# Values and output gates of three heads as one 512-column projection, with the modulation sums kept in their result tiles

## The chip, the cores and the metric

One NeuronCore of one Trainium2 chip runs the whole program. The metric is the device time of one execution in microseconds (us); less is better.

## What is computed

One layer of a backbone over 1024 latent and 256 context tokens, model width 1024, one batch element. `mod` is a vector of six parts of 1024 numbers made from the conditioning vector.

```python
mod = silu(c) @ w_mod + b_mod                 # sh1, sc1, ga1, sh2, sc2, ga2
hc  = modulate(ctx, g_mix, csh1, csc1);  hx = modulate(x, g_mix, sh1, sc1)
p   = h @ w_in                                # q, k, v, o and gates of 4 heads, tokens of hc and hx
# per head: two chunked mLSTM scans (forward, backward), started from the context's state
hn  = h * rsqrt(mean(h*h) + EPS) * gain
y   = (hn * sigmoid(o)) @ w_out;  x = x + ga1 * y
x   = x + ga2 * conv_glu(modulate(x, g_ffn, sh2, sc2))
out = rmsnorm(x, g_final)
```

The head's keys and queries are 128 wide, its values `v` and output gates `o` 256 wide. `o` is needed for the 8 latent chunks alone, `v` for all 10.

## The kernel before

Tokens are cut into 10 chunks of 128: two of context (0, 1) and eight latent (2 to 9). Every product of fp32 numbers is made of three matmuls (`mm3`, L84 to L87: high by high on L85, low by high on L86, high by low on L87), so each weight block is first split into a high and a low half: a copy on ScalarE (L80) and a subtraction on VectorE (L81).

The buffers matter here. Split weights live in tiles with the tag `w`, 8 buffers. Their unsplit sources, and the rows of `w_mod`, land in tiles with the tag `raw`, 3 buffers (`load_raw`, L72); a load into a `raw` tile waits on SyncE's queue (SP) until the tile's last reader is done, and the loads behind it in that queue wait too. Projections accumulate in PSUM tiles `pj`, 2 buffers.

`proj_v` (L278 to L306) makes the values of a head chunk by chunk: 24 matmuls of 256 columns into `pv`, then a copy `vh` (L297, ScalarE) and a rest `vl` (L298, VectorE). `proj_o` makes the output gates of the eight latent chunks in the same way into `po`, with a tanh (L334) and +1 (L335). `proj_qk` makes keys (`pk`) and queries (`pq`) with the roles swapped, 512 tokens at a time. For head 0 the values carry the gate columns along (272 columns), and `gate_rows` turns them into the scan's coefficients: `grp` (L350), `cp` (L387), `bp`, `mp`, `op` on TensorE with VectorE work between, ended by `cco` (L427). `mlstm` then makes per head the two scans: transposed keys `kt`, their scaled halves `kh`/`kl` (L458, L459), chunk states `dc`, scores `s`, outputs `nm`, the normalised `ha` (L545, L551) and its transpose `yp` (L559).

`weave` runs one head's `mlstm` and lets it draw, at some 27 points, units of other matrix work: the values that were left over of this head (`VLATE` = 4 tiles), its output gates, and the next head's keys, queries and first values. Beside every second unit one row of `w_mod` is summed: `mod_sum` (L587 to L596) adds 8 rows of 1024 columns, each times a scalar (L594, VectorE), into a `w` tile that starts at zero. Four such chunks (m3, m4, m2, m5) are made during heads 0 to 2. During head 3 `first_pair` fills in: the gates of head 3, then the output projection of heads 0 and 1 (`opa`) with its weights `wor` (multiplied by ga1, L690, and split) and the y of the heads read back (`load_y`, `split_y` L699/L700), and the residual add (`add_x2`, L711) into x tiles loaded on L727.

The order of instructions on each engine comes out of a scheduler that works on this program with a cost model of its own; the code's order is its input.

Of the kernel before, what the change touches and what calls it, by code (L numbers as in the profile page):

```python
# [9 lines left out]
F32 = mybir.dt.float32  # L10
F32R = mybir.dt.float32r
# [28 lines left out]
def backbone(ctx, tc, x, c, ctxt, c_ctx, w_mod, b_mod, g_mix, g_ffn, w_in, b_gate,  # L40
# [48 lines left out]
    def kp(src):  # L89
        return src.rearrange("(k p) n -> p k n", p=P)  # L90
# [40 lines left out]
    def pj(name):  # L131
        return ps.tile([P, 512], F32, tag="pj", bufs=2, name=name)
# [145 lines left out]
    def proj_v(h, wts=None):  # L278

        hd[h]["v"] = vv = {}  # L280
        if wts is None:
            wh, wl = wcols(OFF_V + h * DV, DV, f"wv{h}_")
            n = DV
        else:
            n = VG
            wh = [a[:, k * n:(k + 1) * n] for a, _ in wts for k in range(4)]
            wl = [a[:, k * n:(k + 1) * n] for _, a in wts for k in range(4)]
        for tt in range(NCH) if wts else BWD:
# [11 lines left out]
            if n == VG:  # L300

                for d, j in ((0, tt), (1, BWD.index(tt))):
                    V.tensor_tensor(out=gt.rearrange("p (y d h) c -> p y d h c", y=2, d=2)[:, :, d, :, j],
                                    in0=p_[:, DV:VG].rearrange("p (y d h) -> p y d h", y=2, d=2)[:, :, d, :],
                                    in1=bgate.rearrange("p (y d h) -> p y d h", y=2, d=2)[:, :, d, :], op=ALU.add)
            yield  # L306

    def proj_qk(h):
# [275 lines left out]
        yield 1  # L584
        readout(LCH - 1)

    def mod_sum(chunk, name, use):  # L587

        acc = wtile(name, F32)
        V.memset(acc, 0.0)  # L590
        nc.sync.dma_start(out=acc[0:1, :], in_=b_mod[:, chunk * D:(chunk + 1) * D])
        for k in range(KT):
            r_ = load_raw(w_mod[k * P:(k + 1) * P, chunk * D:(chunk + 1) * D], f"{name}r{k}")
            V.scalar_tensor_tensor(out=acc, in0=r_, scalar=sct[:, k, 0:1], in1=acc, op0=ALU.mult, op1=ALU.add)  # L594
            yield
# [57 lines left out]
    def along(units, side):  # L653

        for i, _ in enumerate(units):
            if i % 2:
                next(side, None)
            yield

    mods = chain(mod_sum(3, "m3", mod_cols(h2col)), mod_sum(4, "m4", mod_cols(s2col, gffn)),  # L660
                 mod_sum(2, "m2", mod_bcast(ga1)), mod_sum(5, "m5", mod_bcast(ga2)))
    VLATE = 4
    late = iter(())
    for h in range(H - 1):
        nv = proj_v(h + 1)
        fill = along(chain(late, proj_o(h), proj_qk(h + 1), islice(nv, NCH - VLATE)), mods)
        hd[h]["o"] = []
        weave(mlstm(h), fill)
        late = nv
    run(mods)  # L670
# [43 lines left out]

    def first_pair():

        po = proj_o(H - 1)
        yield from islice(po, 4)
        ws = load_wout(0, 0) + load_wout(1, 0)
        yield from po  # L720
        yr = [load_y(0, 0), load_y(0, 1), load_y(1, 0)]
        open_ap()
        ys = [split_y(0, 0, yr[0]), split_y(0, 1, yr[1]), split_y(1, 0, yr[2])]
        ys.append(split_y(1, 1, load_y(1, 1)))
        for tt in range(LCH):
            t_ = atile(f"x2_{tt}")
            nc.sync.dma_start(out=t_, in_=x[tt * P:(tt + 1) * P, :])  # L727
            x2.append(t_)
        for hf in range(2):
            if hf:  # L730
                ws = load_wout(0, 1) + load_wout(1, 1)
            for tt in range(LCH):
                p_ = pj(f"opa_{tt}_{hf}")
                out_mm(p_, tt, ys, ws, True, True)
                add_x2(tt, hf, p_)
                yield
                if hf and tt == 1:
                    wb[1][0] = load_wout(3, 0)
                    wb[0][0] = load_wout(2, 0)

    fill = chain(late, first_pair())
    hd[H - 1]["o"] = []
    weave(mlstm(H - 1), fill)
    y2 = [split_y(2, f, load_y(2, f)) for f in range(2)]
    wb[1][1] = load_wout(3, 1)
# [435 lines left out]
```

## Time and profile before

| | |
|---|---|
| time, three runs | 1227.0, 1227.14, 1228.77 us, median 1227.14 us |
| profiled execution | 1226.6 us, of it a span of 1224.8 us in the trace |
| TensorE (PE) busy | 1190.1 us, 97% of the span, 6395 instructions |
| VectorE (DVE) busy | 887.1 us, 72% |
| ScalarE (ACT) busy | 507.0 us, 41% |
| GpSimd (POOL) busy | 76.6 us, 6% |
| granted TensorE clock, mean | 0.997 of full speed |

How to read it: the span is one profiled execution from first to last instruction. Busy means that an instruction of the engine is under way. In the rows further down, "idle before" stands in square brackets with the instruction that ended the wait, DVE instructions of one engine may overlap by some 0.1 us, and the duration of a matmul is its latency: matmuls overlap, so their pitch is read from start to start.

### The profile page before, as it was taken

What the parts mean: (1) busy time and instruction counts of PE and PEld (TensorE: products, weight loads), DVE (VectorE), ACT (ScalarE), POOL (GpSimd) and SP (SyncE); (2) the same over time, 40 slices, a digit from 0 to 9 for tenths busy, and PEclk for the clock granted to TensorE, in tenths of its full rate; (3) what the DMA queues carried; (4) which work ended last, traced back from release to release, by engine and by line L of the source; (5) the groups of instructions that cost most, each with busy time, mean ns of one, the idle gap of its engine ahead of it and who ended that gap; (6) DMA issues with size and microseconds to landing.
All of it is one profiled execution on the core that took longest, in us unless ns stands there. A gap on an engine that the chain in (4) does not pass through costs nothing. (4 is left out here: it accounts for less than half of the span.)

```text
span 1224.8 us, 17206 instructions
## 1 busy us (share of the span) xinstructions
PE 1190.1 (97%) x6395; PEld 1009.7 (82%) x6395; DVE 887.1 (72%) x1560; ACT 507.0 (41%) x911; POOL 76.6 (6%) x202
## 2 busy tenths in 40 slices
PE   8999999999999999999899999999999999999996
PEld 1788999988998998887678888888888888888885
DVE  3777584776465358657998878788888878986787
ACT  3853354353345335337443333333233344445452
POOL 0100011011001001002500000000000000000011
PEclk9999999999999999999999999999999999999999
DMA  8625252445211115142133222143535469625423
GB/s 322 216 70 157 70 147 86 130 125 155 75 55 59 44 44 223 53 155 104 51 104 103 68 87 96 59 149 128 204 121 189 138 233 401 224 93 167 163 69 120
DMA packets 120020, 160.99 MB, mean 131 GB/s; under 512 B 7932, under 2 KB 81916, under 8 KB 119936
## 3 DMA queue, kind: packets, MB, share of 16 engines
q1 hardware_dynamic: 119936, 159.89, 38.9%
q8 instruction: 50, 0.82, 0.3%
q14 instruction: 34, 0.28, 0.1%
HBM read 125.22 MB, written 34.64 MB: 131 GB/s over the span
## 5 line engine op out<-in xcount | busy, mean ns | idle before, releaser
L912 ACT ACTIVATE t<-gt,cols 128x1024 f32<-128x1024 f32 x22 | 27.4, 1245 | 62.6 <-DVE gt L810 62.6
L810 DVE TENSOR_TENSOR e<-e,p 128x512 f32<-128x512 f32 x66 | 45.1, 685 | 8.4 <-PE p L87 8.3
L810 DVE TENSOR_TENSOR gt<-e,p 128x512 f32<-128x512 f32 x66 | 45.1, 685 | 3.2 <-PE p L87 3.0
L918 ACT ACTIVATE t<-t 128x1024 f32<-128x1024 f32 x22 | 23.4, 1062 | 49.1 <-DVE t L915 49.0
L124 POOL TENSOR_SCALAR fms<-fms 128x1 f32<-128x1 f32 x8 | 3.8, 472 | 607.8 <-PE pa L87 584.3
L551 DVE SCALAR_TENSOR_TENSOR ha<-ha,hms,so 128x256 f32<-128x256 f32 x32 | 15.5, 485 | 33.7 <-POOL hms L125 32.1
L85 PE MATMUL po<-wo_0h,hxh 128*128 128x256 f32 x128 | 37.3, 292 | 0.0
L298 DVE TENSOR_TENSOR vl<-pv,vh 128x256 fp32r<-128x256 f32 x40 | 16.8, 421 | 28.2 <-ACT vh L297 28.0
L85 PE MATMUL pv<-wv_0h,hxh 128*128 128x256 f32 x120 | 34.6, 289 | 2.5 <-DVE vl L298 2.5
L913 DVE SCALAR_TENSOR_TENSOR t<-gt,cols,t 128x960 f32<-128x960 f32 x22 | 26.8, 1217 | 13.3 <-ACT t L912 13.3
L87 PE MATMUL po<-wo_1l,hxh 128*128 128x256 f32 x128 | 36.3, 283 | 0.0
L86 PE MATMUL po<-wo_1h,hxl 128*128 128x256 f32 x128 | 36.2, 283 | 0.0
L85 PE MATMUL po<-wo_1h,hxh 128*128 128x256 f32 x128 | 36.2, 283 | 0.0
L86 PE MATMUL po<-wo_0h,hxl 128*128 128x256 f32 x128 | 36.2, 282 | 0.0
L87 PE MATMUL po<-wo_0l,hxh 128*128 128x256 f32 x128 | 36.2, 282 | 0.0
L85 PE MATMUL pk<-hxh,wk_0h 128*128 128x512 f32 (+1 forms) x96 | 34.3, 358 | 0.0
L85 PE MATMUL p<-bt,av 128*128 128x512 f32 x88 | 34.2, 389 | 0.0
L86 PE MATMUL p<-bt,av 128*128 128x512 f32 x88 | 34.2, 389 | 0.0
L87 PE MATMUL p<-bt,av 128*128 128x512 f32 x88 | 34.2, 389 | 0.0
L86 PE MATMUL pk<-hxh,wk_0l 128*128 128x512 f32 (+1 forms) x96 | 34.2, 356 | 0.0
L87 PE MATMUL pk<-hxl,wk_0h 128*128 128x512 f32 (+1 forms) x96 | 34.0, 355 | 0.0
L87 PE MATMUL pv<-wv_0l,hxh 128*128 128x256 f32 x120 | 34.0, 283 | 0.0
(1031 smaller groups left out, 4247.9 us busy)
## 6 DMA issues: line engine op xcount, KB each, us to landing
rg<-in_f_w_up_dram SPq DMA_DIRECT2D x24, 512.0 KB, 4.3
rv<-in_f_w_up_dram SPq DMA_DIRECT2D x22, 512.0 KB, 3.6
actd<-t SPq DMA_DIRECT2D x22, 512.0 KB, 3.1
dr<-in_f_w_down_dram SPq DMA_DIRECT2D x44, 256.0 KB, 5.1
dr<-sums SPq DMA_DIRECT2D x44, 256.0 KB, 2.9
dr<-actd SPq DMA_DIRECT2D x33, 256.0 KB, 5.1
mr<-in_w_mod_dram SPq DMA_DIRECT2D x16, 512.0 KB, 6.4
sr<-actd SPq DMA_DIRECT2D x11, 512.0 KB, 6.7
```

Of the source, the lines that this page charges most:

```text
L85: T.matmul(ps, ah, bh, start=first, stop=False)
L86: T.matmul(ps, al, bh, start=False, stop=False)
L87: T.matmul(ps, ah, bl, start=False, stop=last)
L124: G.tensor_scalar(out=ms, in0=ms, scalar1=mult / n, scalar2=mult * EPS, op0=ALU.mult, op1=ALU.add)
L298: V.tensor_tensor(out=vl[:, 0:DV], in0=p_[:, :DV], in1=vh[:, 0:DV].bitcast(F32), op=ALU.subtract)
L551: V.scalar_tensor_tensor(out=ha, in0=ha, scalar=ms[:, 1:2], in1=so[i], op0=ALU.mult, op1=ALU.mult)
L810: V.tensor_tensor(out=out_, in0=a_, in1=b_, op=op)
L912: S.activation(out=t_, in_=gate, func=AF.Identity, scale=wcv[:, NFF + ff:NFF + ff + 1], bias=bcv[:, ff:ff + 1])
L913: V.scalar_tensor_tensor(out=t_[:, GRID_W:], in0=gate[:, :SEQ - GRID_W], scalar=wcv[:, ff:ff + 1], in1=t_[:, GRID_W:], op0=ALU.mult, op1=A ...
L918: S.activation(out=t_, in_=t_, func=AF.Silu)
```

## The change

Heads 1 to 3 get `proj_vo` in place of `proj_v` and `proj_o`: one weight block of 512 columns per k holds the head's value columns and its gate columns side by side. For the eight latent chunks 24 matmuls of 512 columns write one `pv` tile, whose first half becomes `vh`/`vl` and whose second half the gate `so`; for the two context chunks it stays at 256 columns. The weights arrive in four `raw` tiles of two loads each (`vor`) and are split into `vo_0` to `vo_3`, which take all eight `w` tiles. Six of the ten tiles are made a head ahead (`EARLY`), the other four, cut in two units each, in the head's own `mlstm`. Head 0 stays as it was. `mod_sum` adds up in `ga1` and `ga2` instead of a `w` tile. `first_pair` loses its eight units of `proj_o`.

```diff
+    def proj_vo(h):
+        hd[h]["v"], hd[h]["o"] = {}, [None] * LCH
+        wts = []
+        for kh in range(KT // 2):
+            r_ = raw_tile(f"vor{h}_{kh}")
...
+            for i, off in enumerate((OFF_V, OFF_O)):
+                nc.sync.dma_start(out=r3[:, :, i * DV:(i + 1) * DV],
+                                  in_=kp(w_in[kh * 2 * P:(kh + 1) * 2 * P, off + h * DV:off + (h + 1) * DV]))
+            h_, l_ = split(r_, f"vo{h}_{kh}")
...
+        for tt in BWD:
+            n = VO if tt >= 2 else DV
+            p_ = pj(f"pv{h}_{tt}")
+            for k in range(KT):
+                mm3(p_[:, :n], hxh[k][:, sl], hxl[k][:, sl], wts[k][0][:, :n], wts[k][1][:, :n], k == 0, k == KT - 1)
+                if k == 3 and tt >= 2:
+                    yield
...
+            S.copy(vh[:, 0:DV], p_[:, :DV])
+            V.tensor_tensor(out=vl[:, 0:DV], in0=p_[:, :DV], in1=vh[:, 0:DV].bitcast(F32), op=ALU.subtract)
+            if tt >= 2:
+                o_ = hp.tile([P, DV], F32, tag="so", bufs=8, name=f"so{h}_{tt}")
+                S.activation(out=o_, in_=p_[:, DV:], func=AF.Tanh, scale=0.5)
+                V.tensor_scalar(out=o_, in0=o_, scalar1=1.0, scalar2=None, op0=ALU.add)
...
-    def mod_sum(chunk, name, use):
-        acc = wtile(name, F32)
+    def mod_sum(chunk, name, use, acc):
         V.memset(acc, 0.0)
...
-    VLATE = 4
+    EARLY = 6
     late = iter(())
     for h in range(H - 1):
-        nv = proj_v(h + 1)
-        fill = along(chain(late, proj_o(h), proj_qk(h + 1), islice(nv, NCH - VLATE)), mods)
-        hd[h]["o"] = []
+        nv = proj_vo(h + 1)
+        if h == 0:
+            hd[0]["o"] = []
+            late = proj_o(0)
+        fill = along(chain(late, proj_qk(h + 1), islice(nv, 2 + 2 * (EARLY - 2))), mods)
         weave(mlstm(h), fill)
...
     def first_pair():
-        po = proj_o(H - 1)
-        yield from islice(po, 4)
         ws = load_wout(0, 0) + load_wout(1, 0)
-        yield from po
+        yield
```

The program order moves with it. Three places are shown; names are those of the code, numbers behind a name only tell two tiles of one name apart, and the code lines of the changed kernel are some 30 further down (its sums are on L625, its `kl` on L491, the values' `vl` of head 0 on L294 and of the others on L331).

The first place is VectorE while the last two chunks of head 0's values are made and the gate chain begins (`it`, `ff` are its first copies, which need `gt` and TensorE's `grp`). Before:

```order
L298 TENSOR_TENSOR vl_8_928<-pv_8_902,vh_8_927 128x256
L303 TENSOR_TENSOR gt<-pv_8_902,bgate 128x2x4 x2
L81 TENSOR_TENSOR wo_0l<-wo_r_1206,wo_0h 128x1024
L81 TENSOR_TENSOR wo_1l<-wo_r_1212,wo_1h 128x1024
L298 TENSOR_TENSOR vl_9_961<-pv_9_935,vh_9_960 128x256
L303 TENSOR_TENSOR gt<-pv_9_935,bgate 128x2x4 x2
L352 COPY it<-grp 40x256
```

And with the change:

```order
L625 SCALAR_TENSOR_TENSOR ga_92<-m3r_1288,vec,ga_92 128x1024
L294 TENSOR_TENSOR vl_8_928<-pv_8_902,vh_8_927 128x256
L298 TENSOR_TENSOR gt<-pv_8_902,bgate 128x2x4 x2
L625 SCALAR_TENSOR_TENSOR ga_92<-m3r_1383,vec,ga_92 128x1024
L81 TENSOR_TENSOR wo_0l<-wo_r_1206,wo_0h 128x1024
L294 TENSOR_TENSOR vl_9_961<-pv_9_935,vh_9_960 128x256
L298 TENSOR_TENSOR gt<-pv_9_935,bgate 128x2x4 x2
L81 TENSOR_TENSOR wo_1l<-wo_r_1212,wo_1h 128x1024
L384 COPY it<-grp 40x256
```

The eight sums of m3, which stood behind `cco`, now stand before and within the gate chain: two ahead of its first copy, six more before `cco`. The loads of rows 1288, 1383 and 1466 follow each other through one `raw` tile.

The second place is VectorE at the turn from head 0 to head 1: the last `ha` of head 0, and `kl` of head 1's first chunks, which the first state `dc` waits for. Before:

```order
L551 SCALAR_TENSOR_TENSOR ha_7_2369<-ha_7_2369,hms_7_2372,so_7_1559 128x256
L298 TENSOR_TENSOR vl_5_2436<-pv_5_2410,vh_5_2435 128x256
L459 SCALAR_TENSOR_TENSOR kl_1_0_2395<-kt_1_0_2392,cco,kh_1_0_2394 128x128
L459 SCALAR_TENSOR_TENSOR kl_1_1_2401<-kt_1_1_2398,cco,kh_1_1_2400 128x128
L459 SCALAR_TENSOR_TENSOR kl_1_2_2444<-kt_1_2_2441,cco,kh_1_2_2443 128x128
```

And with the change:

```order
L583 SCALAR_TENSOR_TENSOR ha_7_2343<-ha_7_2343,hms_7_2346,so_7_1558 128x256
L331 TENSOR_TENSOR vl_7_2365<-pv_7_2307,vh_7_2364 128x256
L625 SCALAR_TENSOR_TENSOR ga_91<-m2r_2971,vec,ga_91 128x1024
L336 TENSOR_SCALAR so_7_2370<-so_7_2370 128x256
L625 SCALAR_TENSOR_TENSOR ga_91<-m2r_3059,vec,ga_91 128x1024
L331 TENSOR_TENSOR vl_6_2409<-pv_6_2373,vh_6_2408 128x256
L491 SCALAR_TENSOR_TENSOR kl_1_0_2427<-kt_1_0_2424,cco,kh_1_0_2426 128x128
```

Two sums stand ahead of `kl`. The next head's `wk_r` and `wq_r` sit in two of the three `raw` tiles there, until `vo_0` and `vo_1` give `w` tiles back; rows 2707, 2875, 2971 and 3059 follow each other through the third.

The third place is VectorE in the middle of head 1, where `vo_3` of head 2 is split. Before, the second half of head 2's value weights stood among other work (`wv_1l`); with the change:

```order
L625 SCALAR_TENSOR_TENSOR ga_92<-m5r_3703,vec,ga_92 128x1024
L556 TENSOR_TENSOR wl_5_3085<-ee_5_3076,wh_5_3084 128x256
L505 SCALAR_TENSOR_TENSOR cf_5_3102<-cf_4_3018,bco,dc_0_5_3098 128x258
L571 SCALAR_TENSOR_TENSOR dn_3_3104<-nm_3_3089,cco 128x2
L557 TENSOR_TENSOR wi_6_3207<-wi_6_3207,qT_1594 128x256
L573 TENSOR_TENSOR dn_3_3104<-nm_3_3089,dn_3_3104 128x2
L547 SCALAR_TENSOR_TENSOR ee_7_3307<-mb_0_3_3208,cco,zmask 128x128
L574 RECIPROCAL dn_3_3104<-dn_3_3104 128x2
L547 SCALAR_TENSOR_TENSOR ee_7_3307<-mb_1_0_3210,cco,zmask 128x128
L625 SCALAR_TENSOR_TENSOR ga_92<-m5r_3764,vec,ga_92 128x1024
L577 SCALAR_TENSOR_TENSOR ha_3_3108<-nm_3_3089,dn_3_3104,ha_3_3108 128x256
L81 TENSOR_TENSOR vo_3l<-vor_3_3151,vo_3h 128x1024
```

`vo_3l` is needed by the 21st of 24 matmuls of the first value tile of head 2 (`pv_1`), and stands behind row 3703, the sixth of eight rows (3189, 3295, 3382, 3462, 3528, 3703, 3837, 4005) that go through one `raw` tile in turn.

## Rows read from the trace of the kernel before

**Rows 1.** The stage of heads 0 and 1, busy time of each engine (share of clock, DMA last)

```profile
110.00:200.00 90.00, 89.14 (x638) 84.03 (x637) 59.22 (x142) 38.97 (x106) 7.14 (x31) 1.00 0.43 130
```

**Rows 2.** Timeline of PE, two streams: 512 columns (pq) and 256 columns (po)

```profile
103.95 0.39 PE L85 MATMUL pq<-hxh,wq_0h 128*128 128x512 f32 x1
...
109.16 0.39 PE L87 MATMUL pq<-hxl,wq_0h 128*128 128x512 f32 x1
...
452.69 0.28 PE L85 MATMUL po<-wo_0h,hxh 128*128 128x256 f32 x1
...
458.32 0.28 PE L87 MATMUL po<-wo_1l,hxh 128*128 128x256 f32 x1
```

**Rows 3.** Waits of PE from 90 to 520 us: total, times, longest

```profile
PE pv L85 <- DVE vl L298: 2.5, 2, 2.0
PE cp L387 <- DVE gs L382: 1.3, 1, 1.3
PE dc L85 <- DVE cb L473: 0.9, 1, 0.9
PE yp L559 <- DVE ha L551: 0.8, 1, 0.8
```

**Rows 4.** Timeline of SP's queue, loads of w_mod (x2, x3: several issues in one row)

```profile
71.77 11.63 SPq L72 DMA_DIRECT2D m3r<-in_w_mod_dram  x3
...
284.67 5.15 SPq L72 DMA_DIRECT2D m5r<-in_w_mod_dram  x2
...
291.82 0.33 SPq L72 DMA_DIRECT2D m5r<-in_w_mod_dram  x1
...
299.08 0.33 SPq L72 DMA_DIRECT2D m5r<-in_w_mod_dram  x1
```

**Rows 5.** Timeline of DVE: the sums that take those loads

```profile
288.17 1.29 DVE L594 SCALAR_TENSOR_TENSOR m<-m5r,vec,m 128x1024 f32<-128x1024 f32 x1 [1.02 <-DMA m5r<-in_w_mod_dram]
...
297.77 1.28 DVE L594 SCALAR_TENSOR_TENSOR m<-m5r,vec,m 128x1024 f32<-128x1024 f32 x1 [2.34 <-DMA m5r<-in_w_mod_dram]
...
303.34 1.28 DVE L594 SCALAR_TENSOR_TENSOR m<-m5r,vec,m 128x1024 f32<-128x1024 f32 x1 [3.16 <-DMA m5r<-in_w_mod_dram]
```

**Rows 6.** Groups of DVE instructions, 90 to 520 us: busy, mean ns, idle before

```profile
L594 DVE SCALAR_TENSOR_TENSOR m<-m5r,vec,m 128x1024 f32<-128x1024 f32 x8 | 10.3, 1283 | 7.8 <-DMA m5r<-in_w_mod_dram 7.8
...
L81 DVE TENSOR_TENSOR wv_0l<-wv_r,wv_0h 128x1024 fp32r<-128x1024 f32 x3 | 3.7, 1224 | 0.4 <-PE po L86 0.3
```

**Rows 7.** Timeline of DVE at five places

```profile
83.29 0.17 DVE L303 TENSOR_TENSOR gt<-pv,bgate 128x8 f32<-128x8 f32 x1
...
205.43 0.48 DVE L551 SCALAR_TENSOR_TENSOR ha<-ha,hms,so 128x256 f32<-128x256 f32 x1 [1.55 <-POOL hms L125]
...
207.41 0.35 DVE L459 SCALAR_TENSOR_TENSOR kl<-kt,cco,kh 128x128 fp32r<-128x128 f32 x1 [1.16 <-ACT kh L458]
...
469.69 0.68 DVE L711 TENSOR_TENSOR x<-x,opa 128x512 f32<-128x512 f32 x1
...
512.80 0.48 DVE L551 SCALAR_TENSOR_TENSOR ha<-ha,hms,so 128x256 f32<-128x256 f32 x1 [1.54 <-POOL hms L125]
```

**Rows 8.** Timeline of PE at five places

```profile
83.61 0.27 PE L350 MATMUL grp<-ident,gt 128*40 128x128 f32 x1
...
205.97 0.33 PE L559 MATMUL yp<-ident,ha 128*128 128x128 f32 x1 [0.81 <-DVE ha L551]
...
207.95 0.28 PE L86 MATMUL dc<-vh,kl 128*128 128x258 f32 x1
...
508.74 0.28 PE L87 MATMUL nm<-vl,wh 128*128 128x258 f32 x1
...
588.47 0.68 PE L85 MATMUL p<-ba,ag2h 128*128 128x512 f32 x1 [3.89 <-ACT ag2h L80]
```

**Rows 9.** Windows behind a stop of PE, as rows 1

```profile
588.00:590.00 2.00, 1.53 (x4) 1.25 (x5) 2.00 (x2) 1.98 (x4) 1.08 (x1) 0.66 0.00 0
590.00:592.00 2.00, 2.00 (x7) 1.52 (x6) 2.00 (x5) 0.00 (x0) 0.00 (x0) 0.50 0.00 0
```

More of the change, by code (lines that the diff above doesn't have):

```diff
@@ L276, in backbone, with proj_v @@
     hd = [dict() for _ in range(H)]
-    def proj_v(h, wts=None):
+    def proj_v(h, wts):
         hd[h]["v"] = vv = {}
[L281 to L288, printed above, removed]
+        n = VG
+        wh = [a[:, k * n:(k + 1) * n] for a, _ in wts for k in range(4)]
+        wl = [a[:, k * n:(k + 1) * n] for _, a in wts for k in range(4)]
+        for tt in range(NCH):
             sl = slice(tt * P, (tt + 1) * P)
@@ L299, in proj_v @@
             vv[tt] = vh, vl
[L300 to L305, printed above, removed]
+            for d, j in ((0, tt), (1, BWD.index(tt))):
+                V.tensor_tensor(out=gt.rearrange("p (y d h) c -> p y d h c", y=2, d=2)[:, :, d, :, j],
+                                in0=p_[:, DV:VG].rearrange("p (y d h) -> p y d h", y=2, d=2)[:, :, d, :],
+                                in1=bgate.rearrange("p (y d h) -> p y d h", y=2, d=2)[:, :, d, :], op=ALU.add)
@@ new lines, in proj_v @@
+            yield
+    VO = 2 * DV
+    def proj_vo(h):
[3 more added lines that the diff above has]
+            r_ = raw_tile(f"vor{h}_{kh}")
+            r3 = r_.rearrange("p (k n) -> p k n", k=2)
+            for i, off in enumerate((OFF_V, OFF_O)):
+                nc.sync.dma_start(out=r3[:, :, i * DV:(i + 1) * DV],
+                                  in_=kp(w_in[kh * 2 * P:(kh + 1) * 2 * P, off + h * DV:off + (h + 1) * DV]))
+            h_, l_ = split(r_, f"vo{h}_{kh}")
+            wts += [(h_[:, k * VO:(k + 1) * VO], l_[:, k * VO:(k + 1) * VO]) for k in range(2)]
+        for tt in BWD:
+            sl = slice(tt * P, (tt + 1) * P)
+            n = VO if tt >= 2 else DV
[4 more added lines that the diff above has]
+                    yield
+            vh = vp.tile([P, VG], F32R, tag="vh", bufs=NCH, name=f"vh{h}_{tt}")[:, :DV + 2]
+            vl = vp.tile([P, VG], F32R, tag="vl", bufs=NCH, name=f"vl{h}_{tt}")[:, :DV + 2]
+            G.memset(vh[:, DV:].bitcast(F32), 1.0)
+            G.memset(vl[:, DV:].bitcast(F32), 0.0)
+            S.copy(vh[:, 0:DV], p_[:, :DV])
+            V.tensor_tensor(out=vl[:, 0:DV], in0=p_[:, :DV], in1=vh[:, 0:DV].bitcast(F32), op=ALU.subtract)
+            hd[h]["v"][tt] = vh, vl
+            if tt >= 2:
+                o_ = hp.tile([P, DV], F32, tag="so", bufs=8, name=f"so{h}_{tt}")
+                S.activation(out=o_, in_=p_[:, DV:], func=AF.Tanh, scale=0.5)
+                V.tensor_scalar(out=o_, in0=o_, scalar1=1.0, scalar2=None, op0=ALU.add)
+                hd[h]["o"][tt - 2] = o_
@@ L658, in along @@
             yield
-    mods = chain(mod_sum(3, "m3", mod_cols(h2col)), mod_sum(4, "m4", mod_cols(s2col, gffn)),
-                 mod_sum(2, "m2", mod_bcast(ga1)), mod_sum(5, "m5", mod_bcast(ga2)))
-    VLATE = 4
+    mods = chain(mod_sum(3, "m3", mod_cols(h2col), ga2), mod_sum(4, "m4", mod_cols(s2col, gffn), ga2),
+                 mod_sum(2, "m2", mod_bcast(ga1), ga1), mod_sum(5, "m5", mod_bcast(ga2), ga2))
+    EARLY = 6
     late = iter(())
     for h in range(H - 1):
-        nv = proj_v(h + 1)
-        fill = along(chain(late, proj_o(h), proj_qk(h + 1), islice(nv, NCH - VLATE)), mods)
-        hd[h]["o"] = []
+        nv = proj_vo(h + 1)
[3 more added lines that the diff above has]
+        fill = along(chain(late, proj_qk(h + 1), islice(nv, 2 + 2 * (EARLY - 2))), mods)
         weave(mlstm(h), fill)
@@ L715, in first_pair @@
     def first_pair():
-        po = proj_o(H - 1)
-        yield from islice(po, 4)
         ws = load_wout(0, 0) + load_wout(1, 0)
-        yield from po
+        yield
         yr = [load_y(0, 0), load_y(0, 1), load_y(1, 0)]
@@ L741, in backbone @@
     fill = chain(late, first_pair())
-    hd[H - 1]["o"] = []
     weave(mlstm(H - 1), fill)
```

## The prediction, made before the changed kernel ran

> **What bounds the kernel now.** I read four views. The windows by stage come first: in the stage of heads 0 and 1 TensorE is busy 89.14 of 90 us [rows 1], so whatever it is spared shows in the time, and so does every new wait of it. The timeline of TensorE gives the pitch of its matmuls [rows 2]. The list of its waits says what stops it now: 5.5 us between 90 and 520 us, all of them behind VectorE [rows 3]. The timelines of SP's queue and of VectorE show why VectorE is late: sums of rows of `w_mod` wait for a load [rows 4 to 6]. The sum below is made against the profiled execution, 1226.6 us; the median of the runs is 0.5 above it. A difference of 0.2%, 2.45 us, is about what a measurement of this kernel can tell.
>
> **Fewer matmuls.** Eight chunks of three heads need 24 matmuls of 512 columns in place of 48 of 256: 576 pairs become single ones. The 256-column stream has 48 matmuls from 452.69 to 458.32, 47 steps of 0.1198 us; the 512-column stream 24 from 103.95 to 109.16, 23 steps of 0.2265 us [rows 2]. A pair costs 0.2396, so each gives back 0.0131, and 576 give **7.5 us**, all on the path of TensorE by rows 1; I take 7.4, since four more steps into a tile change weights at a yield. Nothing else bounds it from below but a pitch as long as the pair's, no gain.
> The Trainium skill, page "TensorE: Matmul & The Clock Gate", section "Back-to-back issue gap", gives an isolated matmul a gap of N/2.4 + 2.5 ns, by which a pair costs 215.8 + 2.5 + 2.5 against 215.8 + 2.5 and the change gives back 576 x 2.5 ns, an estimate of 1.4 us. The trace differs: 13.1 ns a pair.
>
> **Edits at nothing.** ScalarE and VectorE do the same instructions; tanh and +1 of a chunk come right behind its `vh` and `vl`. SP has four loads of 256 KB per head more, beside an idle queue. The store of the gate maxima now stands behind the `vor` loads on SP, some 8 us later; its readers are needed by the first scores, for which TensorE has gates of head 0 and states to do first. The memsets that move to the start are off the path.
>
> **Waits that go.** The sums of m3 and m5 stand elsewhere now, the turn to head 1 has more filler, so the 2.5, 1.3, 0.9 and 0.8 us of rows 3 go: **-5.5 us**. Their causes come back at other places:
>
> **A load and its sum as a link.** Row for row, the sums of a chunk now share one `raw` tile in turn at the three places shown with the change. A load can start only when the sum before it is done. From issue to the waiting sum it takes 3.50 us (284.67 to 288.17), 4.26 (299.08 to 303.34) or 5.95 (291.82 to 297.77) [rows 4, 5]. I take the middle one, 4.26; with 1.28 for the sum [rows 6] a link is 5.57 us. VectorE works in order, so all behind such a sum waits too.
>
> *First place, gates.* The load of row 1288 starts at 71.77 as now [rows 4], lands at 76.1 and is summed by 77.4. Row 1383 lands at 81.7, is summed by 83.0, and then come the split of `wo_0` (1.22), `vl_9` and the gates: done at 84.8, where now it is 83.5 (83.29 and two of 0.17) [rows 7]. TensorE stands at `grp` three matmuls of 512 columns earlier than now, 83.61 - 0.68 = 82.9 [rows 8]: a stop of 1.9. Six more sums (7.7) and a split (1.22) lie within the chain that follows; it has 1.9 us more of idle stretches to hide them in at each table load of ScalarE, and `cp` comes 22 matmuls later in TensorE's order. Following both, TensorE waits 1.1 at `cp` and 0.4 at `bp`. Together **3.4**; with loads of 3.50 I get 1.3, with 5.95 about 10.
>
> *Second place, the turn to head 1.* Now `ha` of the last chunk starts at 205.43 and `kl` at 207.41, 1.98 later [rows 7], and the state `dc` with it at 207.95 [rows 8]. With the change `vl_7`, a sum, a load, a sum and `vl_6` lie between: 0.4 + 0.4 + 1.28 + 4.26 + 1.28 + 0.4 = 8.0, which is 6.0 more. Against it stands that `ha` is ready before TensorE asks for `yp_7`: between `nm_7` and `yp_7` lie 36 matmuls of 512 columns, 8.2 us, while the chain from `nm_7` to the end of `ha` took 4.5 in head 3 (508.74 to 512.80 and 0.48) [rows 7, 8]. But VectorE has thirteen sums (16.7) beside its own work there and hardly idles, so I leave 1.1 of the 3.7. Price **4.9**; ends 6.0 - 0.8 - 3.7 = 1.5 and 6.0 + 1.7 = 7.7.
>
> *Third place, `vo_3` in head 1.* From the end of sum 3189, which comes at `nm_0`, to that of 3703 are five links, 27.9; the eleven rows to the end of `vo_3l`, a sum and a split [rows 6] and nine of some 0.25, take 4.6: 32.5. TensorE has 72 matmuls of 512 columns (16.3), 44 of 256 (5.3) and four steps of scores, `nm` and `dc` (13 or 14 matmuls of up to 258 columns, 1.6 each at 0.12) up to the 21st matmul of `pv_1`, less 1.4 that passed before: 27. Price **5.5**; with loads of 3.50 VectorE's own work sets it, 3.0; with 5.95 up to 13.
>
> *`vo_3` in heads 0 and 2*, without sums: its `w` tiles come free with the last `pq` matmul, then a copy on ScalarE and 1.22 [rows 6] against 20 matmuls of 0.12: 0.4 each, **0.8**; ends 0 and 2.4.
>
> *Hand-over to `opa`.* The gate tiles of head 3 lay among its first scores; now its last value tile is followed by the splits of `wor` and of four y at once. The first residual add came 11.4 us after the last `po` matmul (458.32, 469.69) [rows 2, 7]; two more splits, 2.4, stand before it, and the x loads behind both `wor` loads on SP start some 2 us later. TensorE has no other work: **2.0**, ends 0 (all beside) and 6.0, a whole load of 5.95.
>
> *End of head 3.* Eight fill units are gone, so one `opa` tile is left behind `nm_7` where there were three: 12 x 0.2265 = 2.7 against the 4.5 of the chain, to which a split of y (1.22) is added. **3.0**, ends 1.8 and 4.5.
>
> *Clock.* Behind a stop of 3.89 us [rows 8] the granted clock was 0.66 and then 0.50 of full, its lower level of 1.2 GHz, for 2 us each [rows 9]: 0.7 + 1.0 = 1.7 us of work lost. The second and third stop are longer: **3.4**; ends 0 and 5.1.
>
> **Sum.** -7.4 - 5.5 + 3.4 + 4.9 + 5.5 + 0.8 + 2.0 + 3.0 + 3.4 = +10.1: 1236.7, on the runs' median **1237 us**, slower by 0.8%. All low ends: -12.9 + 7.6 = -5.3, 1222. The high ends together pass 1260, but they don't meet.
>
> **Rivals.** *Short stops.* The sum crosses zero when the three places cost 12.9 - 5.8 = 7.1 us together instead of 13.8, and no clock falls. With loads of 3.50 and VectorE ahead at the turn they cost 1.3 + 1.5 + 3.0, and the time is 1226.6 - 12.9 + 11.6 = 1225.3, 1226 on the median; with the low ends of the rest too it is 1222. For it: the row of 3.50. Against it: the two other rows, and that two loads now often run side by side. I give 0.15 to the stretch within 0.2% and 0.10 to faster.
> The Trainium skill, page "DMA: Bandwidth & Descriptors", section "Anatomy of one DMA", has about 2.0 us and bytes / 436e9 s per transfer, an estimate of 3.2 us for 512 KB, by which this rival would hold. Rows 4 and 5 show none as short.
>
> *The sums are covered.* VectorE may be far enough ahead of TensorE that the three places stop nothing, as most of the 7.8 us that the m5 sums wait now do no harm [rows 3, 6]. Left are 0.8, 2.0 and 3.0: 1226.6 - 12.9 + 5.8 = 1219.5, with the median 1220. Against it: `kl` and `vo_3l` are needed within some 2 us. 0.05.
>
> *Long loads.* At 5.95 the three places alone cost 31, and the time passes 1249: 0.08.
>
> *No gain from width.* If one of 512 columns cost the pair's time, only the waits stay: 1237 + 7.4 = 1244. Against it: rows 2. 0.03. The Trainium skill's issue gap, above, comes near this: an estimate of 1243.
>
> That the matmuls don't go is ruled out by the order: TensorE has 576 fewer.
>
> **How the numbers follow.** The forecast's own case, 1230 to 1249, has 0.59. Slower: 0.59 + 0.08 + 0.03 = 0.70; within 0.2%: 0.15; faster: 0.10 + 0.05 = 0.15. The range from 1222 to 1249 leaves out some 0.08 on each side. The likeliest case alone is 1230 to 1249.
>
> **What would show it.** Right: `pv` of 512 columns at a pitch of 0.2265; TensorE's waits grow from 5.5 to some 20 us, of which `grp`, `dc` behind `kl` at the turn to head 1 and `pv` behind `vo_3l` in head 1 are over 1.5, 3 and 3 us; VectorE's waits of `ga` for m3, m2 and m5 rows some 20 us in all. Wrong: `kl` of head 1 within 3 us behind `ha`; sums that wait less than in rows 6; no lower clock behind the stops.

## The result, and the profile after

| | before | with the change |
|---|---|---|
| median of the runs beside each other | 1227.07 us (4) | 1235.93 us (4: 1233.52, 1234.41, 1237.46, 1239.06) |
| ratio | | 1.0071, 95% interval 1.0054 to 1.0087 |
| profiled execution, its span | 1226.6, 1224.8 us | 1233.52, 1231.7 us |
| TensorE matmuls in the trace | 6395 | 5819 |
| granted clock, mean of the profiled execution | 0.997 | 0.990 |

Slower by 0.7%, where 0.8% was forecast: 1235.9 against 1237. The profiled execution is the fastest of the four, so the account below is of 6.9 us and not of 8.9. From the page's first part, of the changed kernel (busy us, share of the span, instructions):

```profile
PE 1190.1 (97%) x5819; PEld 981.8 (80%) x5819; DVE 888.2 (72%) x1560; ACT 508.8 (41%) x911; POOL 71.6 (6%) x202
```

TensorE's busy time is what it was, 1190.1 us, with 576 matmuls fewer. That looks as if the wider matmuls had brought nothing. They did, as the starts of one value tile of 512 columns show (timeline of TensorE, head 1's values made beside head 0; the first column is the start, the second the latency):

```profile
198.03 0.39 PE L85 MATMUL pv<-vo_2h,hxh 128*128 128x512 f32 x1
198.26 0.39 PE L86 MATMUL pv<-vo_2h,hxl 128*128 128x512 f32 x1
...
203.25 0.39 PE L87 MATMUL pv<-vo_1l,hxh 128*128 128x512 f32 x1
```

23 steps in 5.22 us, 0.227 each. Over the nine whole tiles of this kind that nothing interrupts the mean is 0.2277, and over the 21 uninterrupted 256-column tiles (`pv`, `po`) of before it is 0.1198, 0.2395 a pair. So each pair that became one matmul gave back 0.0118 us, 576 of them **6.8 us**. The busy time hides this, because time at the lower clock is busy time too.

Now the waits of TensorE between 60 and 530 us, which answer to [rows 3] (total, times, longest):

```profile
PE yp L591 <- DVE ha L583: 3.2, 1, 3.2
PE dc L86 <- DVE kl L491: 3.1, 1, 3.1
PE nm L566 <- DVE ha L577: 2.5, 2, 1.4
PE opa L85 <- DVE x L744: 2.2, 1, 2.2
PE opb L85 <- DVE yl L602: 1.2, 1, 1.2
PE cp L419 <- DVE gs L414: 0.7, 1, 0.7
...
PE pv L87 <- DVE vo_3l L81: 0.6, 1, 0.6
...
PE grp L382 <- DVE gt L298: 0.4, 1, 0.4
PE opa L86 <- DVE yl L733: 0.2, 1, 0.2
```

Together with the two lines not shown (0.7 and 0.5) this list comes to 15.3 us. The list of before over the same stretch comes to 7.2: the four lines of [rows 3], the same 0.7 and 0.5, and 0.5 at `opa`. That is **+8.1**. Nearly all of it stands behind VectorE, and in new places: head 1's first state (`dc` behind `kl`), the end of head 3 (`yp`, then `opb`), the hand-over to `opa`.

The third item is the clock. Windows of the changed kernel in four stretches (busy of each engine, then granted clock, DMA share, GB/s), as in [rows 9]:

```profile
466.00:468.00 2.00, 1.61 (x5) 1.32 (x6) 2.00 (x7) 0.41 (x1) 0.00 (x0) 0.78 1.03 420
468.00:470.00 2.00, 2.00 (x6) 1.51 (x6) 1.32 (x7) 0.78 (x2) 0.00 (x0) 0.50 1.02 418
...
526.00:528.00 2.00, 2.00 (x6) 1.58 (x5) 1.15 (x3) 1.09 (x2) 0.00 (x0) 0.50 0.80 233
...
596.00:598.00 2.00, 2.00 (x6) 1.52 (x6) 2.00 (x4) 0.71 (x2) 0.00 (x0) 0.50 0.00 0
...
608.00:610.00 2.00, 2.00 (x6) 1.54 (x5) 2.00 (x4) 0.00 (x0) 0.00 (x0) 0.50 0.68 205
```

A window at 0.50 is at the lower level, 1.2 GHz, and loses 1 us of work. With the windows beside them the four stretches lose 1.7, 1.7, 3.4 and 1.7 us, 8.5 together; before lost 1.7 at one place in the same range. **+6.8**, at most: 0.9 of the 3.4 lies within a stop that lasts to 595.20, where there was no work to lose.

Only half of it stands beside the new stops of head 3, though. The last two stretches lie in `conv_glu`, which the change does not touch. TensorE waits 3.9 us for `ag2h` there in both kernels; the fall around that stop took 3.4 us before and 6.8 us in this execution, and the wait that follows it is longer (first line before, second with the change):

```profile
PE p L86 <- DVE ag2l L81: 0.9, 1, 0.9
PE p L86 <- DVE ag2l L81: 3.4, 1, 3.4
```

Why that fall was longer is open; the profiled executions of held_apart and held_more, below, have the long fall without this wait.

The three items and the waits outside 60 to 530 us close the account of the two profiled executions. All waits of TensorE in the lists over the whole spans come to 24.5 us before and 31.1 after, +6.6 (so 1.5 less outside 60 to 530 us: 2.5 more at `ag2l`, 4.0 less at several others). Then -6.8 + 6.6 + 6.8 = +6.6, and the spans differ by 6.9. With the 0.9 taken off, 1.2 us stay unaccounted for.

### The profile page after: what moved, and what is told of

The parts are those of the page before. It is cut to its first block, busy times and chain, and to the rows that moved or that the text cites. A ratio compares the mean times of both kernels' runs of the same rounds, so it can differ in the third digit from the quotient of the medians.

```text
span 1231.7 us, 16096 instructions
## 1 busy us (share of the span) xinstructions
PE 1190.1 (97%) x5819; PEld 981.8 (80%) x5819; DVE 888.2 (72%) x1560; ACT 508.8 (41%) x911; POOL 71.6 (6%) x202
## 4 chain that ended last, share of the span: by engine, by line
PE 49%; DVE 3%; ACT 0%; POOL 0%; issue 0%; DVEq 0%; POOLq 0%; ACTq 0%
PE p L86 11%; PE p L87 11%; PE p L85 11%; PE pa L85 3%; PE pa L86 3%; PE pa L87 3%; PE pb L87 2%; PE pb L85 2%; PE pb L86 2%; DVE bt L823 1%; DVE dr L1131 0%; DVE bs L840 0%; DVE bu L823 0%; DVE at0l L81 0%; DVE dr L840 0%
## 5 line engine op out<-in xcount | busy, mean ns | idle before, releaser
L943 DVE SCALAR_TENSOR_TENSOR t<-gt,cols,t 128x960 f32<-128x960 f32 x22 | 26.7, 1216 | 13.4 <-ACT t L942 13.3
L331 DVE TENSOR_TENSOR vl<-pv,vh 128x256 fp32r<-128x256 f32 x30 | 12.5, 418 | 28.2 <-ACT vh L330 28.2
L549 ACT ACTIVATE wi<-mb,bco 128x128 f32<-128x128 f32 x64 | 23.6, 398 | 15.4 <-PE nm L566 15.3
L85 PE MATMUL nm<-vh,wh 128*128 128x258 f32 x64 | 29.9, 467 | 0.0
L330 ACT CAST vh<-pv 128x256 fp32r<-128x256 f32 x30 | 11.1, 370 | 43.1 <-PE pv L87 42.8
L491 DVE SCALAR_TENSOR_TENSOR kl<-kt,cco,kh 128x128 fp32r<-128x128 f32 x44 | 14.9, 346 | 17.7 <-ACT kh L490 17.7
L576 ACT ACTIVATE ha<-nm,dn 128x256 f32<-128x256 f32 x32 | 15.1, 473 | 29.7 <-DVE dn L574 29.6
L945 DVE SCALAR_TENSOR_TENSOR t<-gt,cols,t 128x960 f32<-128x960 f32 x22 | 26.7, 1212 | 0.0
L840 DVE TENSOR_TENSOR sa<-rv 128x512 f32<-128x512 f32 x22 | 15.1, 688 | 15.0 <-DMA rv<-in_f_w_up_dram 15.0
L86 PE MATMUL pq<-hxh,wq_0l 128*128 128x512 f32 x64 | 25.2, 394 | 0.0
```

Of the source, the lines that this page charges most:

```text
L85: T.matmul(ps, ah, bh, start=first, stop=False)
L86: T.matmul(ps, al, bh, start=False, stop=False)
L491: V.scalar_tensor_tensor(out=kl, in0=tp[:, c0:c0 + P], scalar=wc, in1=kh.bitcast(F32), op0=ALU.mult, op1=ALU.subtract)
L549: S.activation(out=wi[:, d, :], in_=mrow_, func=AF.Exp, scale=-1.0, bias=mpco[:, cc:cc + 1])
L576: S.mul(ha, nm[:, 0, :DV], dn[:, 0, :])
L840: V.tensor_tensor(out=out_, in0=a_, in1=b_, op=op)
```

## Where the waits come from

The turn from head 0 to head 1, VectorE of the changed kernel (start, duration; in brackets the idle time before it), to be held against [rows 7]:

```profile
210.94 0.48 DVE L583 SCALAR_TENSOR_TENSOR ha<-ha,hms,so 128x256 f32<-128x256 f32 x1 [1.55 <-POOL hms L125]
211.35 0.42 DVE L331 TENSOR_TENSOR vl<-pv,vh 128x256 fp32r<-128x256 f32 x1
211.98 1.28 DVE L625 SCALAR_TENSOR_TENSOR ga<-m2r,vec,ga 128x1024 f32<-128x1024 f32 x1 [0.21 <-DMA m2r<-in_w_mod_dram]
...
217.77 1.29 DVE L625 SCALAR_TENSOR_TENSOR ga<-m2r,vec,ga 128x1024 f32<-128x1024 f32 x1 [4.30 <-DMA m2r<-in_w_mod_dram]
...
219.31 0.60 DVE L491 SCALAR_TENSOR_TENSOR kl<-kt,cco,kh 128x128 fp32r<-128x128 f32 x2
```

and TensorE, which waits for that `kl`:

```profile
219.71 0.39 PE L86 MATMUL dc<-vh,kl 128*128 128x258 f32 x1 [3.11 <-DVE kl L491]
```

From `ha` to `kl` it is 8.4 us, 1.98 before. The chain is the forecast one: a sum ends at 213.26, only then can the load into the same `raw` tile start, and the next sum has its data at 217.77, 4.5 later. `kl` itself needs no load; it stands behind the sum on an engine that works in order.

The hand-over and the end of head 3 have another cause. SP's queue, VectorE and TensorE of the changed kernel at the hand-over, one fence each:

```profile
456.29 1.81 SPq L72 DMA_DIRECT2D wor<-in_a_w_out_dram  x2
458.19 6.43 SPq L758 DMA_DIRECT2D x<-in_x_dram  x8
```

```profile
465.65 0.69 DVE L744 TENSOR_TENSOR x<-x,opa 128x512 f32<-128x512 f32 x1 [2.53 <-DMA x<-in_x_dram]
```

```profile
462.18 0.70 PE L566 MATMUL nm<-cf,wi 128*128 128x258 f32 x2 [1.39 <-DVE ha L577]
...
466.39 0.50 PE L85 MATMUL opa<-wow_0h,yh 128*128 128x512 f32 x1 [2.24 <-DVE x L744]
...
523.78 0.44 PE L591 MATMUL yp<-ident,ha 128*128 128x128 f32 x2 [3.24 <-DVE ha L583]
525.44 0.79 PE L85 MATMUL opb<-wow_0h,yh 128*128 128x512 f32 x1 [1.22 <-DVE yl L602]
```

The x tiles are asked for behind the loads of `wor` and arrive 7.5 us later; no gate tile is left to fill that time. The 1.39 at `nm` just before has four splits of y (1.2 us each, from 452.14 on) ahead of `ha` on VectorE. At the end of head 3 nothing but one `opa` tile covers the chain from `nm_7` to `yp_7`.

## The experiments

All were timed in five rounds beside the kernel before. Its median there was 1226.7 (narrow to head3_apart), 1227.2 (the three held kernels) and 1229.3 us (the last two), so kernels of different groups are compared by their ratios to it (0.001 is 1.2 us). Diffs are against the changed kernel unless it is said otherwise.

**1. narrow: what the width is worth.** Only the matmuls of `proj_vo` are cut in two again; order, loads, tiles and all else stay.

```diff
-                mm3(p_[:, :n], hxh[k][:, sl], hxl[k][:, sl], wts[k][0][:, :n], wts[k][1][:, :n], k == 0, k == KT - 1)
+                for c0 in range(0, n, DV):
+                    cs = slice(c0, c0 + DV)
+                    mm3(p_[:, cs], hxh[k][:, sl], hxl[k][:, sl], wts[k][0][:, cs], wts[k][1][:, cs],
+                        k == 0 and c0 == 0, k == KT - 1 and c0 + DV == n)
```

> The changed kernel with each 512-column matmul of the joined projection cut into two of 256 columns on the same weights; all else as in the changed kernel, so 576 matmuls come back. If the width saves what the two streams of the trace of before show (0.0131 us a pair), this is slower than the changed kernel by up to 7.5 us: 1241 to 1244, less the part in which TensorE would have stood waiting anyway (the stop before dc at the turn to head 1 should shrink from 3.1 to about 1 us, as TensorE comes later). If a wide matmul saves only 2.5 ns a pair, as an isolated one would by the rule cited in the prediction, it is 1236 to 1238.

Measured 1241.13 us, ratio 1.0112 (1.0098 to 1.0125), 0.0041 or 5.0 us above the change; the profiled spans are 7.9 apart (1239.6 and 1231.7). In its trace the twelve uninterrupted runs of 48 value matmuls step by 0.1198 us, the change's nine whole tiles by 0.2277: 2 x 0.1198 - 0.2277 = 0.0119, times 576 is 6.9. So the wider matmul gives back some 5 to 8 us of time. One part of the expectation failed: the stop before `dc` did not shrink to 1 us, it stayed at 3.0. TensorE came later to the turn, but so did the `ha` at which VectorE's chain begins (212.05 instead of 210.94). The prediction's figure stands, and the 1.4 us that it had worked out from the Trainium skill, page "TensorE: Matmul & The Clock Gate", section "Back-to-back issue gap", does not.

**2. noload: the links of load and sum.** The sums take a tile that is resident anyway, so no load stands in their way; the kernel leaves out the loads and with them the real values of the later modulation.

```diff
-            r_ = load_raw(w_mod[k * P:(k + 1) * P, chunk * D:(chunk + 1) * D], f"{name}r{k}")
+            r_ = hxl[k][:, 0:D].bitcast(F32)
```

> The changed kernel with the 32 sums of the later modulation reading a resident tile in place of a freshly loaded row of w_mod: the loads are left out, the sums stay on VectorE. If the loads through one raw tile make the new stops of heads 0 and 1, the waits of TensorE at cp, nm, dc (3.1) and pv in heads 0 and 1 go, some 5.5 us in all, and the time is 1229 to 1231; the stops at the hand-over to opa and at the end of head 3 stay. If VectorE's own work with the sums makes them, dc still waits over 2 us and the time stays above 1234.

Measured 1228.49, ratio 1.0011 (1.0001 to 1.0021): 0.0060 or 7.4 us below the change, 0.5 below the range expected. Its longest waits of TensorE from 60 to 530 us:

```profile
PE yp L591 <- DVE ha L583: 3.2, 1, 3.2
PE opa L85 <- DVE x L744: 2.0, 1, 2.0
PE nm L566 <- DVE ha L577: 1.7, 2, 1.3
PE opb L85 <- DVE yl L602: 1.2, 1, 1.2
```

`dc`, `cp`, `grp` and `vo_3l` are gone from the list, the hand-over and the end of head 3 stay within 0.2. A limit of this run: without loads the scheduler also places the sums elsewhere, so it takes away the links and their places together. What the kernel before would gain without these loads was not measured.

**3. sums_only: the second half of the change alone.** The kernel before, with the sums in their result tiles (diff against before):

```diff
-    def mod_sum(chunk, name, use):
+    def mod_sum(chunk, name, use, acc):
-        acc = wtile(name, F32)
...
-    mods = chain(mod_sum(3, "m3", mod_cols(h2col)), mod_sum(4, "m4", mod_cols(s2col, gffn)),
+    mods = chain(mod_sum(3, "m3", mod_cols(h2col), ga2), mod_sum(4, "m4", mod_cols(s2col, gffn), ga2),
```

> The kernel before with the second part of the change alone: the sums add up in their result tiles, the projections stay apart. If sums that the scheduler moves ahead of the next head's kl are what stops TensorE at the turn, this is slower than before by 2 to 4 us (1229 to 1231) with a wait at dc of 1 to 3 us in head 1. If the accumulator's place is harmless and the joined projection alone makes the stops, it is within 1.5 us of 1227.

Measured 1229.54, ratio 1.0021 (1.0010 to 1.0031). Taking the sums out of a `w` tile costs 2.6 us by itself, as forecast, but not by the wait that was forecast. VectorE's waits for rows of `w_mod` grow from 10.5 us (60 to 530 us, before) to 17.5, and new waits show on TensorE (1.86 at `nm` behind `ha`); as many others went, and TensorE's total over that stretch is 7.1 us, against 7.2 before. So its waits don't account for the 2.6, and the cause of it is not shown. The stop at `dc` behind `kl` is not among them; it came only with both halves of the change.

**4. head3_apart: the gate tiles as filler.** Heads 1 and 2 as in the change, head 3 with `proj_v` and `proj_o` as before, its gates in `first_pair` again.

```diff
-        nv = proj_vo(h + 1)
+        nv = proj_vo(h + 1) if h < H - 2 else proj_v3(h + 1)
...
+        po = proj_o(H - 1)
+        yield from islice(po, 4)
         ws = load_wout(0, 0) + load_wout(1, 0)
-        yield
+        yield from po
```

> The changed kernel with head 3 as before, values and gates apart, so that the gate tiles of head 3 again lie among its first scores and at its end three opa tiles are left. If the missing fill makes the stops at the hand-over (2.2 and 1.4) and at the end of head 3 (3.2 and 1.2) and with them two falls of the clock (1.7 each), they go, and 192 pairs cost 2.5 more: 1236 - 8 - 3.4 + 2.5 + 0.5 = 1227 to 1229. If those stops come from the weights of the output projection or the x loads, 1233 or more.

Measured 1228.75, ratio 1.0022 (1.0011 to 1.0032): 0.0049 or 6.0 us below the change (7.2 by the medians), although a third of the width's gain is given up. Its longest waits of TensorE:

```profile
PE dc L86 <- DVE kl L521: 2.8, 1, 2.8
PE nm L596 <- DVE ha L607: 1.2, 1, 1.2
...
PE opa L85 <- DVE x L774: 0.4, 1, 0.4
```

The mirror image of noload: the turn stays, hand-over and end are gone.

**5. noload_apart: both at once.**

> Both suspects at once: the sums take a resident tile in place of the loaded rows of w_mod (the 32 loads and the real values of the later modulation are left out), and head 3 keeps values and gates apart. Alone the first gave 1228.49 and the second 1228.75 against 1235.9 of the change, 7.4 and 7.2 us less. Theory (the two groups of stops are separate: the links of load and sum cost the turn to head 1, cp and vo_3; the missing gate units cost the hand-over and the end of head 3; each with its lower clock): they add, 1235.9 - 7.4 - 7.2 = 1221.3, taken as 1220 to 1223, some 5 us below the kernel before, which is what the width gives; TensorE's waits from 60 us to the first opb under 5 us. Rival (both runs got back the same thing, a lower clock that either stop alone brings on): 1227 to 1229, and waits of 2 us or more left over at the turn or at the hand-over.

Measured 1221.05, ratio 0.9936 (0.9917 to 0.9955). By the ratios the two edits alone took 0.0060 and 0.0049 off 1.0071, which would leave 0.9962; both took off 0.0135. They add within the intervals, so the two groups of stops are separate. No wait of TensorE between 60 and 530 us is over 0.8 us. The 0.6% gained on the kernel before is not the worth of the width alone, which is 4.5 us for two heads: TensorE's waits in that stretch are 3.3 us here and 7.2 there, and the 32 loads, which this run leaves out, delay sums in the kernel before too.

**6. held: the sums out of the turn.** In heads 1 and 2 rows are drawn from the 10th fill unit on only.

```diff
-            if i % 2:
+            if (i % 2 if h == 0 else i >= 9 and i % 2):
                 next(side, None)
```

> The changed kernel with the sums of heads 1 and 2 drawn only from the tenth fill unit on (every second unit), so that no two sums through one raw tile stand before kl of head 1; the joined projection stays in all three heads. If the pair of sums in that place makes the stop of 3.1 us before dc, it falls below 1 us and the time is 1231 to 1233.5 (3 us less than the changed kernel, the stops at the hand-over and at the end of head 3 stay). If the stop comes from the joined tiles themselves (vl, so and tanh behind one another), dc still waits 2 us or more and the time stays above 1234.

A miss in the time: 1235.74, ratio 1.0060 (1.0041 to 1.0078). The stop at `dc` is gone, as meant. But the list of its waits shows where it went:

```profile
PE yp L591 <- DVE ha L583: 4.3, 2, 3.2
...
PE pv L87 <- DVE vo_3l L81: 1.8, 2, 1.1
...
PE pv L85 <- ACT vo_3h L80: 1.3, 2, 0.7
```

`yp` now waits 1.1 at the turn, and TensorE waits for `vo_3` in heads 1 and 2, 3.1 in four places. In head 1 it is the rows that come later: two sums (at 277.73 and 282.41) stand ahead of `vo_3`. In head 2 it is not a sum: VectorE's last one ends at 378.8, and two multiplications of `wor` by ga1 (1.2 us each, at 379.88 and 382.80) stand there. Taking the sums from one place does not take them from VectorE.

**7. held_apart and held_more: a version that beats both.** held with head 3 apart, as in 4. Then another cadence: in head 0 rows only up to the 20th unit, in heads 1 and 2 two in three units from the 10th on.

```diff
-            if i % 2:
+            if (i % 2 and i < 20 if h == 0 else i >= 9 and i % 3):
```

> Both cures together: sums held back as in the run before and head 3 with values and gates apart. If the two groups of stops are independent, the savings add: head 3 apart was 1228.75, less some 3 us and, where the clock falls behind that stop, 1.7 more: 1223 to 1226, level with or up to 0.3% faster than the kernel before. If one stop only takes the place of another, 1227 to 1229.

> As the run before, but no sums in the last seven units of head 0 either and two in three units of heads 1 and 2, so that fewer sums fall into head 0's last chunks, where nm waits 1.1 us for ha. If that wait is VectorE's own queue of sums, it goes and the time is about 1 us below the run before; otherwise they are alike within 1 us.

held_apart measured 1225.24, ratio 0.9985 (0.9975 to 0.9994), held_more 1224.62, ratio 0.9973 (0.9961 to 0.9985): faster than the kernel before by 0.27%, and by 0.0098 or 12 us faster than the change. The three longest waits of held_more:

```profile
PE pv L85 <- ACT vo_3h L80: 0.9, 1, 0.9
PE yp L621 <- DVE ha L613: 0.8, 1, 0.8
PE pv L87 <- DVE vo_3l L81: 0.8, 1, 0.8
```

Two thirds of the width's 6.8 would be 4.5, and 3.3 is what is left on top of the kernel before when the links are put where little waits for them. The two versions are not told apart, as their intervals overlap; and the wait of 1.1 at `nm` from which held_more set out is 0.2 in held_apart's trace already. That savings add, as held_apart was to show, is not exact either: held alone took 0.0011 off, and beside head3_apart 0.0037, a difference that the intervals just allow.

**8. early_chunks: one step further, a miss.** As held_more, with two in three units carrying a row in head 0 up to the 17th.

```diff
-            if (i % 2 and i < 20 if h == 0 else i >= 9 and i % 3):
+            if (i % 3 if h == 0 and i < 17 else h and i >= 9 and i % 3):
```

> As held_more (head 3 apart, sums held back to the 10th fill unit in heads 1 and 2, two in three units there), and in head 0 two in three units up to the 17th carry a sum, so that vo_3 of head 2 no longer stands in a chain of m5 rows in the program order; the last m5 rows then come later in head 2. Theory (a wait of TensorE behind VectorE is wherever a link of load and sum stands just ahead of what TensorE needs next): the waits for vo_3l in head 1 go (0.75 in held_more), no stop at the turn, 1223 to 1225. Rival (the links only move again, as in held against the change): another stop of 1 to 3 us, in head 0 where the sums now stand closer or ahead of head 3, and 1225 to 1229.

Measured 1231.5, ratio 1.0020 (1.0007 to 1.0033). The rival held, with a time above its range. TensorE:

```profile
PE pv L85 <- ACT vo_3h L80: 2.2, 1, 2.2
PE cp L449 <- DVE gs L444: 2.1, 1, 2.1
```

The denser rows of head 0 stand in the gate chain, and the stop at `cp` grows from 0.7 to 2.1. In head 1 a sum that waits for its load (0.99 us, at 281.18) holds up VectorE's small steps (`dn`) that ScalarE needs for `ha`; ScalarE idles 3.2 us, and the copy `vo_3h` stands behind that in ScalarE's order. So the sum stops TensorE through an engine that does no sum.

## Why the prediction was right, point by point

The sum came out at +10.1 against the profiled execution, which stands 6.9 above it, and the forecast of the median 1.1 above the measured one. The mechanism and the sign were right: the three kinds of new wait are in the trace, and taking them away (experiments 2, 4 and 5) turns the change to the good. Several terms were not the right size, though, and errors of both signs cancelled: the three places cost 4.8 us together instead of 13.8, the clock, the end of head 3 and two waits that were not in the sum made up for most of it. That the time came within 1.1 us is luck.

| term | forecast | measured in the profile |
|---|---|---|
| fewer matmuls | -7.4 | -6.8 |
| waits of before that go | -5.5 | -5.5 |
| first place, gates (`grp`, `cp`, `bp`) | 3.4 | 0.4 + 0.7 |
| turn to head 1 (`dc` behind `kl`) | 4.9 | 3.1 |
| `vo_3` in head 1 | 5.5 | 0.6 |
| `vo_3` in heads 0 and 2 | 0.8 | 0 |
| hand-over to `opa` | 2.0 | 2.2 + 0.2 |
| end of head 3 | 3.0 | 3.2 + 1.2 |
| not in the sum: `nm` behind `ha`, at 196 and 462 us | | 1.1 + 1.4 |
| lower clock | 3.4 | 6.8, half of it in `conv_glu` |

*Width.* Right, by the pitch and by experiment 1. The 0.6 too much comes from the tile that I took for the 512-column pitch: 0.2265 there, 0.2277 in the mean. (Two slips of the prediction change nothing: 512 / 2.4 is 213.3 ns, not 215.8, and 4.26 + 1.28 is 5.54, not 5.57.)

*Waits that go.* Right: none of the four of [rows 3] is left as it was. `cp` is counted with the first place, and the `yp` that waits now is another one, at the end of head 3.

*First place: mis-sized by 2.3.* The order of events is the forecast one, but the loads were quicker. VectorE's sums at the gates in the changed kernel:

```profile
75.70 1.29 DVE L625 SCALAR_TENSOR_TENSOR ga<-m3r,vec,ga 128x1024 f32<-128x1024 f32 x1 [0.62 <-DMA m3r<-in_w_mod_dram]
...
80.51 1.28 DVE L625 SCALAR_TENSOR_TENSOR ga<-m3r,vec,ga 128x1024 f32<-128x1024 f32 x1 [1.68 <-DMA m3r<-in_w_mod_dram]
...
83.18 0.23 DVE L298 TENSOR_TENSOR gt<-pv,bgate 128x8 f32<-128x8 f32 x2
```

From the end of the first sum to the second it took 3.5 us, not 4.26, and the load before it (issued at 71.79) 3.9; so `gt` is done at 83.4 instead of 84.8, and `grp` waits 0.4. I had worked out 1.3 for loads of 3.50, and 1.1 is what came. The estimate of 3.2 us for 512 KB from the Trainium skill, page "DMA: Bandwidth & Descriptors", section "Anatomy of one DMA", is nearer here than the row that I took; at the turn, with 4.5 us, it is not. That section gives its formula for transfers that GpSimd issues, which the prediction did not say; these go through SyncE's queue.

*Turn to head 1: right in the chain, 1.8 too much.* `ha` to `kl` took 8.4 us, forecast 8.0. TensorE had more of the filler left than the 1.1 us that I left it, so 3.1 of it shows. A link at `nm_6` (two sums in front of `ha`, 1.07 at 196.01) came on top, which I had not listed.

*`vo_3` in head 1: the step that failed.* VectorE's side came out near: from the end of the sum of row 3189 (253.76) to the end of `vo_3l` (285.53) it took 31.8 us, forecast 32.5. But in two of the five links (the sums at 258.01 and 274.91) VectorE's other work was longer than the load, and it waited for loads only 2.0 us in all, so this length is as much that work as the links. The failure is TensorE's side: "16.3 + 5.3 + four steps of scores at 1.6, less 1.4", 27. The window of TensorE from that sum to the moment at which it began to wait is

```profile
253.76:284.96 31.20, 31.20 (x185) 1.00 0.52 160
```

31.2 us of work without a gap. The 72 and 44 fill matmuls are there as counted (21.6). The four steps are 69 matmuls, not 54, since each chunk has two directions of `nm` and transposes besides; they take 9.6, not 6.4, and the 1.4 that I took off had no ground. So the cover nearly reached, and the stop was 0.62. The lesson is that a stop is a small difference of two long stretches, and both want counting from the trace.

*Hand-over and end: right* (the end 1.4 too little), and experiment 4 shows that the missing gate units are the cause. What I missed is that the same pile of work on VectorE (four splits of y) also delays head 3's own `ha`, 1.39 at `nm`, and that `opb` waits 1.2 behind `yp`.

*Clock: right in kind, mis-sized and misplaced.* I put it behind the second and the third stop; in the profiled execution it fell behind the hand-over, behind the end of head 3 and, as before the change, in `conv_glu`, where it lost 5.1 instead of 1.7. Over all executions the size can be read from their mean granted clocks: 0.994 before (mean of 69 executions beside the experiments) and 0.989 with the change (mean of 4); 0.005 of 1230 us is some 6 us of work. That would be most of the 8.9 us by which the medians differ, while waits and width nearly cancel. noload had 0.9914, head3_apart 0.9927 and noload_apart 0.9948: in these three the clock comes back as the stops go. It does not follow them one for one, as held_more has fewer waits than the kernel before (5.6 against 7.2 us from 60 to 530) and a mean of 0.9926. In the same way 0.0024 and 0.0037 of 1230, 3.0 and 4.6 us, are an estimate of the clock's share in what noload (7.4 us) and head3_apart (6.0 us) won.

*What was to show it.* The pitch is there, and the stops over 1.5 and 3 us are there for `dc` but not for `grp` and `vo_3l`. VectorE's waits for rows of m3, m2 and m5 are 10.6 us, not some 20, as VectorE had other work meanwhile and the loads that it did wait for mostly took 3.4 to 4.5 us (one 5.3); the total of waits on an engine that is off the path says little of the time.

*The rivals.* "Short stops" had its 3.50 us loads at the gates, but the turn, the hand-over and the end were not short. "The sums are covered" falls by the 3.1 at `dc`, though it came near at the other two places (1.1 and 0.6). "Long loads" falls by those 3.4 to 4.5 us. "No gain from width" falls by experiment 1.

## What to carry to other kernels

Merging two projections takes matmuls away, but it also takes away work that can be moved: ask which long chains the removed units stood beside, and leave the merge out where they were the only cover (here head 3). A sum that shares one buffer with the next row's load is a link of load and sum; place such links where the engine's next few results are not awaited, since moving them off one spot puts them in front of another. And where TensorE is 97% busy, add 1.7 us, the size of most falls here, to a stop of 2 us or more for the lower clock that may follow it.

## What was not expected of the hardware

Whether the clock falls is not settled by the length of the stop. Behind the stop at `dc` the change's granted clock stayed at 1.00 (3.11 us, first fence), while narrow's fell behind nearly the same stop (3.04, second fence); behind the hand-over it was the other way round (2.24 in the change, which fell to 0.50 as shown above, and 2.19 in narrow, last line).

```profile
220.00:222.00 2.00, 2.00 (x13) 1.70 (x13) 0.89 (x4) 0.37 (x1) 0.00 (x0) 1.00 0.84 256
```

```profile
222.00:224.00 2.00, 2.00 (x11) 2.00 (x10) 0.00 (x0) 0.17 (x1) 0.00 (x0) 0.50 0.47 152
...
474.00:476.00 2.00, 1.65 (x7) 1.39 (x8) 2.00 (x7) 0.41 (x1) 0.00 (x0) 1.00 1.00 412
```

Nor is the length of the fall: after the 2.25 us stop at 285.56 in early_chunks the clock was still at 0.50 eight us later, with TensorE at work nearly all the time. A window of early_chunks:

```profile
292.00:294.00 2.00, 2.00 (x8) 1.81 (x8) 0.99 (x3) 0.80 (x3) 0.00 (x0) 0.50 0.48 142
```

A fall does not even need a stop. In head3_apart's profile the clock fell at 179.5 us, 77 us after the last wait of TensorE that the lists hold (0.17 us, at 102.13). Just before stand sixteen matmuls of 2 columns, first line; the second is a window behind them. The other kernels run the same sixteen, and in none of their profiles did the clock fall there.

```profile
177.03 1.84 PE L663 MATMUL mcp<-ones,ga 128*128 128x2 f32 x16
...
180.00:182.00 2.00, 2.00 (x9) 1.81 (x8) 1.01 (x4) 0.32 (x2) 0.00 (x0) 0.50 0.24 68
```

Executions of one and the same kernel differ in this: mean clocks of 0.991 to 0.996 for held_more, with times from 1220.8 to 1227.3 us. What decides it within one execution stays open; no run here tells it apart.
